# Rotary embedding on one core: float32 transfers on SyncE's queue, rotated in place in five buffers

## The chip, the cores and the metric

The kernel runs on one core of a Trainium2 chip. The metric is the device time of one execution in microseconds (us); the median of eleven runs before the change is 322.9 us, with 321.63 the lowest and 323.37 the highest. Five engines of the core matter here: VectorE (DVE in the profile), ScalarE (ACT), GpSimd (POOL), SyncE (SP), and the 16 DMA engines that move data between HBM and SBUF. TensorE does nothing in this kernel.

## The reference

A rotary position embedding. Each head of 64 numbers is split into two halves, and the halves are rotated by the angle of their place in the sequence:

```python
batch, seq_len, num_heads, head_dim = (8, 2048, 16, 64)
# x: (8, 2048, 16, 64) float32; cos, sin: (2048, 32) float32
x1 = x[..., :head_dim // 2]
x2 = x[..., head_dim // 2:]
out1 = x1 * cos - x2 * sin
out2 = x1 * sin + x2 * cos
return np.concatenate([out1, out2], axis=-1).astype(np.float32)
```

The input and the output are 67.11 MB each; each table is 0.26 MB. Each number of x is used once.

## The kernel before

The work is cut into 16 tiles: two halves of the sequence (1024 rows each) by eight batches, with the half of the sequence as the outer loop. In a tile each of the 128 partitions holds J = 8 consecutive rows of the sequence, which are 8 x 16 x 64 = 8192 numbers. In HBM these are 32 KB in one piece for each partition.

Lines 37 and 38 load the tables cos and sin into SBUF once, as float16. Then each pass of the loop at line 40 does this:

- Line 44 loads a tile of x into the buffer `xt`. The load is issued from GpSimd's queue (`nc.gpsimd.dma_start`), and the transfer turns float32 into float16 on its way.
- Line 59 multiplies the whole tile by cos into `ot`. Lines 65 and 66 multiply the two halves by sin into `v1` and `v2`. Lines 69 and 70 subtract and add these, in place in `ot`. All five run on VectorE in float16. The table is repeated over the heads by its access pattern.
- Line 72 stores `ot`, again from GpSimd's queue, and the transfer turns float16 into float32.

The pools (lines 29 to 31) keep three buffers of each of `xt`, `ot`, `v1` and `v2`. So a load needs that VectorE has read the tile three before it to the end (line 66 is the last reader), and line 59 needs that the store three before it has landed.

The kernel is written on a framework that places the waits and chooses the order of the instructions on each engine; the order in the text is a wish. Each engine then works its own queue off strictly in order, and an instruction that waits holds up what stands behind it on that engine. A transfer's issue is such an instruction, too. What is issued goes into a DMA queue, and one transfer is spread over all 16 DMA engines.

Of the kernel before, what the change touches and what calls it, by code (L numbers as in the profile page):

```python
# [1 line left out]

# [4 lines left out]


@with_exitstack  # L10
def kernel(
    ctx: ExitStack,
    tc: tile.TileContext,
    x: bass.AP,
    cos: bass.AP,
    sin: bass.AP,
    out: bass.AP,
):
    nc = tc.nc
    f16 = mybir.dt.float16  # L20

    B, S, H, D = x.shape
    Dh = D // 2
    P = nc.NUM_PARTITIONS
    J = 8
    NT = S // (J * P)
    T2 = J * P

    const_pool = ctx.enter_context(tc.tile_pool(name="rope_const", bufs=1))
    io_pool = ctx.enter_context(tc.tile_pool(name="rope_io", bufs=3))  # L30
    tmp_pool = ctx.enter_context(tc.tile_pool(name="rope_tmp", bufs=3))

    cos_src = cos.rearrange("(t p j) d -> p t (j d)", p=P, j=J)
    sin_src = sin.rearrange("(t p j) d -> p t (j d)", p=P, j=J)
    cos_sb = const_pool.tile([P, NT, J * Dh], f16)
    sin_sb = const_pool.tile([P, NT, J * Dh], f16)
    nc.gpsimd.dma_start(out=cos_sb, in_=cos_src)  # L37
    nc.gpsimd.dma_start(out=sin_sb, in_=sin_src)  # L38

    for it in range(NT * B):  # L40
        t, b = divmod(it, B)
        s0 = T2 * t
        xt = io_pool.tile([P, J, H, D], f16)
        nc.gpsimd.dma_start(  # L44
            out=xt,
            in_=x[b, s0 : s0 + T2].rearrange("(p j) h d -> p (j h d)", j=J),
        )

        ot = io_pool.tile([P, J, H, D], f16)
        v1 = tmp_pool.tile([P, J, H, Dh], f16)  # L50
        v2 = tmp_pool.tile([P, J, H, Dh], f16)

        x1 = xt[:, :, :, 0:Dh]
        x2 = xt[:, :, :, Dh:D]

        cos_b = cos_sb[:, t, :].rearrange("p (j d) -> p j d", d=Dh).unsqueeze(2)
        sin_b = sin_sb[:, t, :].rearrange("p (j d) -> p j d", d=Dh).unsqueeze(2)

        nc.vector.tensor_mul(  # L59
            out=ot.rearrange("p j h (e d) -> p j (h e) d", d=Dh),  # L60
            in0=xt.rearrange("p j h (e d) -> p j (h e) d", d=Dh),
            in1=cos_b.to_broadcast([P, J, 2 * H, Dh]),
        )
        sin_bb = sin_b.to_broadcast([P, J, H, Dh])
        nc.vector.tensor_mul(out=v1, in0=x2, in1=sin_bb)  # L65
        nc.vector.tensor_mul(out=v2, in0=x1, in1=sin_bb)  # L66
        o1 = ot[:, :, :, 0:Dh]
        o2 = ot[:, :, :, Dh:D]
        nc.vector.tensor_sub(out=o1, in0=o1, in1=v1)  # L69
        nc.vector.tensor_add(out=o2, in0=o2, in1=v2)  # L70

        nc.gpsimd.dma_start(  # L72
            out=out[b, s0 : s0 + T2].rearrange("(p j) h d -> p (j h d)", j=J),
            in_=ot,
        )


# [1 line left out]
_INS = ['x', 'cos', 'sin']  # L79
_OUTS = [((8, 2048, 16, 64), 'float32')]  # L80


# [23 lines left out]
```

## Time and profile before

| What | us |
|---|---|
| Median of 11 runs | 322.9 |
| The profiled execution, its own time | 323.28 |
| Its span in the profile | 321.0 |
| VectorE busy, 80 instructions | 210.7 |
| VectorE idle ahead of line 59, for loads of x | 93.0 |
| GpSimd idle for line 70 (ahead of a store) | 166.9 |
| GpSimd idle for line 66 (ahead of a load) | 117.6 |
| Issue to landing, loads of x, median | 24.3 |
| Issue to landing, stores, median | 20.4 |

The span is the time from the first to the last instruction that the profile holds; the execution's own time is 2.3 us longer. "Issue to landing" includes the time that a transfer waits behind others in the queue. The profile counts the bytes of a transfer where they are written, so that a load, which becomes float16, counts 2 MB and a store 4 MB, though both move 4 MB at the HBM. A rate of some 215 GB/s in a stretch of loads and of some 430 GB/s in a stretch of stores are thus the same rate at the HBM.

### The profile page before, as it was taken

How to read it: one execution, taken by the hardware profiler on the slowest of the kernel's cores; microseconds unless marked ns; L12 is line 12 of the kernel's file. 1: busy time of each engine (PE TensorE's matmuls, PEld its weight loads, DVE VectorE, ACT ScalarE, POOL GpSimd, SP SyncE). 2: the span in 40 equal slices, each digit the busy share in tenths (PEclk: the TensorE clock that was granted, in tenths of full speed). 3: DMA queues.
4: the chain of work that ended last, by engine and by line, in shares of the span. 5: the costliest groups of instructions: out<-in, count | busy, mean ns of one | idle time of the engine just before them, and what ended most of it. 6: DMA issues, size and time to landing. Idle time of an engine off the chain costs nothing.

```text
span 321.0 us, 191 instructions
## 1 busy us (share of the span) xinstructions
DVE 210.7 (66%) x80; POOL 18.9 (6%) x38
## 2 busy tenths in 40 slices
DVE  0079999980009999995003999999100799999800
POOL 4001000011000100002000000000200010000000
DMA  6999999999999999999999999999999999999994
GB/s 88 210 206 227 210 276 425 441 437 421 337 216 212 223 212 359 441 416 449 437 239 225 212 214 234 421 437 433 425 402 212 216 220 214 294 437 421 449 433 196
DMA packets 5154, 100.94 MB, mean 314 GB/s; under 512 B 545, under 2 KB 1057, under 8 KB 1057
## 3 DMA queue, kind: packets, MB, share of 16 engines
q0 software_dynamic: 5152, 100.93, 100.1%
q14 instruction: 2, 0.01, 0.0%
HBM read 67.63 MB, written 67.11 MB: 420 GB/s over the span
## 4 chain that ended last, share of the span: by engine, by line
DVE 45%; DMA 27%; issue 20%; POOL 2%; POOLq 0%; DVEq 0%; PEldq 0%
DMA xt<-in_x_dram 27%; DVE ot L59 16%; DVE v L66 8%; DVE v L65 8%; DVE ot L70 8%; DVE ot L69 4%; POOL out_dram L72 1%; POOL cos_sb L37 0%; POOL sin_sb L38 0%; POOLq L101 0%; POOL xt L44 0%; POOLq L72 0%; DVEq L59 0%; PEldq L101 0%; POOLq L44 0%
## 5 line engine op out<-in xcount | busy, mean ns | idle before, releaser
L59 DVE TENSOR_TENSOR ot<-xt,cos_sb 128x8192 f16<-128x8192 f16 x16 | 70.7, 4421 | 93.0 <-DMA xt<-in_x_dram 92.9
L66 DVE TENSOR_TENSOR v<-xt,sin_sb 128x4096 f16<-128x4096 f16 x16 | 36.6, 2285 | 0.0
L69 DVE TENSOR_TENSOR ot<-ot,v 128x4096 f16<-128x4096 f16 x16 | 36.6, 2285 | 0.0
L70 DVE TENSOR_TENSOR ot<-ot,v 128x4096 f16<-128x4096 f16 x16 | 36.6, 2285 | 0.0
L65 DVE TENSOR_TENSOR v<-xt,sin_sb 128x4096 f16<-128x4096 f16 x16 | 36.6, 2284 | 0.0
L72 POOL DMA_DIRECT2D out_dram<-ot x16 | 8.6, 536 | 166.9 <-DVE ot L70 166.9
L44 POOL DMA_DIRECT2D xt<-in_x_dram x16 | 8.6, 549 | 117.6 <-DVE v L66 117.6
L37 POOL DMA_DIRECT2D cos_sb<-in_cos_dram x1 | 0.8, 827 | 0.8 <-PEq L101 0.8
L38 POOL DMA_DIRECT2D sin_sb<-in_sin_dram x1 | 0.7, 728 | 0.0
L90 POOL MEMSET const-float32-0.0<- 128x1 f32 x1 | 0.1, 99 | 0.2 <-issue 0.2
L90 POOL MEMSET const-bfloat16-1.0<- 128x1 bf16 x1 | 0.1, 102 | 0.0
L90 POOL MEMSET const-float32-1.0<- 128x1 f32 x1 | 0.1, 99 | 0.0
L90 POOL MEMSET const-uint8-127<- 128x1 uint8 x1 | 0.1, 99 | 0.0
## 6 DMA issues: line engine op xcount, KB each, us to landing
out_dram<-ot POOLq DMA_DIRECT2D x16, 4096.0 KB, 20.4
xt<-in_x_dram POOLq DMA_DIRECT2D x16, 2048.0 KB, 24.3
cos_sb<-in_cos_dram POOLq DMA_DIRECT2D x1, 128.0 KB, 3.3
sin_sb<-in_sin_dram POOLq DMA_DIRECT2D x1, 128.0 KB, 3.1
```

Of the source, the lines that this page charges most:

```text
L37: nc.gpsimd.dma_start(out=cos_sb, in_=cos_src)
L38: nc.gpsimd.dma_start(out=sin_sb, in_=sin_src)
L44: nc.gpsimd.dma_start(out=xt, in_=x[b, s0 : s0 + T2].rearrange("(p j) h d -> p (j h d)", j=J),)
L59: nc.vector.tensor_mul(out=ot.rearrange("p j h (e d) -> p j (h e) d", d=Dh), in0=xt.rearrange("p j h (e d) -> p j (h e) d", d=Dh), in1=cos ...
L65: nc.vector.tensor_mul(out=v1, in0=x2, in1=sin_bb)
L66: nc.vector.tensor_mul(out=v2, in0=x1, in1=sin_bb)
L69: nc.vector.tensor_sub(out=o1, in0=o1, in1=v1)
L70: nc.vector.tensor_add(out=o2, in0=o2, in1=v2)
L72: nc.gpsimd.dma_start(out=out[b, s0 : s0 + T2].rearrange("(p j) h d -> p (j h d)", j=J), in_=ot,)
L90: nc = _bacc.Bacc("TRN2", target_bir_lowering=False, num_devices=1)
```

## The change

All transfers are now plain float32 copies, issued from SyncE's queue. The conversion to float16 and back is done by ScalarE in SBUF. A partition holds J = 16 consecutive rows of a batch's sequence (64 KB in HBM), and a unit is half of these, JU = 8 rows (32 KB for each partition); there are 16 units, two for each batch. A unit is computed in two pieces of JC = 4 rows.

- `load` brings a unit into one of five float32 buffers `xf` (NBUF = 5). Four loads are issued ahead, and the tables are loaded as float32 behind the first of them and turned into float16 by ScalarE.
- `narrow` (ScalarE) copies a piece into a float16 tile, of which there are three. `rotate` (VectorE) does the five operations of before on half as many numbers; the product with cos, the difference and the sum are now written in place into this tile. `widen` (ScalarE) copies the result back as float32 into the same place of `xf`.
- The narrowing of the next piece stands ahead of the rotation of this one in the text.
- When both pieces of unit u are done, the text issues the load of unit u + 4, and then the store of unit u out of its `xf`. Unit u + 4 takes the buffer of unit u - 1, whose store must have landed.

```diff
-    J = 8
-    NT = S // (J * P)
-    T2 = J * P
+    J = S // P
+    JU = 8
+    JC = 4
+    NBUF = 5
...
-    io_pool = ctx.enter_context(tc.tile_pool(name="rope_io", bufs=3))
-    tmp_pool = ctx.enter_context(tc.tile_pool(name="rope_tmp", bufs=3))
+    io_pool = ctx.enter_context(tc.tile_pool(name="rope_io", bufs=NBUF))
+    half_pool = ctx.enter_context(tc.tile_pool(name="rope_half", bufs=3))
+    tmp_pool = ctx.enter_context(tc.tile_pool(name="rope_tmp", bufs=1))
...
-    nc.gpsimd.dma_start(out=cos_sb, in_=cos_src)
-    nc.gpsimd.dma_start(out=sin_sb, in_=sin_src)
...
-        xt = io_pool.tile([P, J, H, D], f16)
-        nc.gpsimd.dma_start(
-            out=xt,
-            in_=x[b, s0 : s0 + T2].rearrange("(p j) h d -> p (j h d)", j=J),
-        )
...
+    def load(u):
+        b, j0 = units[u]
+        xf = io_pool.tile([P, JU, H, D], f32)
+        nc.sync.dma_start(out=xf.rearrange("p j h d -> p (j h d)"), in_=rows(x, b, j0))
+        return xf
 
+    def store(u, xf):
+        b, j0 = units[u]
+        nc.sync.dma_start(out=rows(out, b, j0), in_=xf.rearrange("p j h d -> p (j h d)"))
...
+    def narrow(c):
+        xt = half_pool.tile([P, JC, H, D], f16)
+        nc.scalar.copy(out=xt.rearrange("p j h d -> p (j h d)"), in_=piece(c))
+        halves[c] = xt
...
+    def rotate(c):
...
+        nc.vector.tensor_mul(out=v1, in0=x2, in1=sin_b)
+        nc.vector.tensor_mul(out=v2, in0=x1, in1=sin_b)
+        xw = xt.rearrange("p j h (e d) -> p j (h e) d", d=Dh)
+        nc.vector.tensor_mul(out=xw, in0=xw, in1=cos_b)
+        nc.vector.tensor_sub(out=x1, in0=x1, in1=v1)
+        nc.vector.tensor_add(out=x2, in0=x2, in1=v2)
...
+    def widen(c):
+        xt = halves.pop(c)
+        nc.scalar.copy(out=piece(c), in_=xt.rearrange("p j h d -> p (j h d)"))
...
+    for u in range(NBUF - 1):
+        tiles[u] = load(u)
+        if u == 0:
+            nc.sync.dma_start(out=sin_f, in_=sin.rearrange("(p j) d -> p j d", j=J))
+            nc.sync.dma_start(out=cos_f, in_=cos.rearrange("(p j) d -> p j d", j=J))
+            nc.scalar.copy(out=sin_sb, in_=sin_f)
+            nc.scalar.copy(out=cos_sb, in_=cos_f)
 
+    narrow(0)
+    for c in range(n * per):
+        if c + 1 < n * per:
+            narrow(c + 1)
+        rotate(c)
+        widen(c)
+        if c % per == per - 1:
+            u = c // per
+            if u + NBUF - 1 < n:
+                tiles[u + NBUF - 1] = load(u + NBUF - 1)
+            store(u, tiles[u])
...
-        nc.gpsimd.dma_start(
-            out=out[b, s0 : s0 + T2].rearrange("(p j) h d -> p (j h d)", j=J),
-            in_=ot,
-        )
```

More of the change, by code (lines that the diff above doesn't have):

```diff
@@ L20 @@
     f16 = mybir.dt.float16
+    f32 = mybir.dt.float32
     B, S, H, D = x.shape
@@ L24 @@
     P = nc.NUM_PARTITIONS
-    J = 8
-    NT = S // (J * P)
-    T2 = J * P
+    J = S // P
+    JU = 8
+    JC = 4
+    NBUF = 5
     const_pool = ctx.enter_context(tc.tile_pool(name="rope_const", bufs=1))
-    io_pool = ctx.enter_context(tc.tile_pool(name="rope_io", bufs=3))
-    tmp_pool = ctx.enter_context(tc.tile_pool(name="rope_tmp", bufs=3))
-    cos_src = cos.rearrange("(t p j) d -> p t (j d)", p=P, j=J)
-    sin_src = sin.rearrange("(t p j) d -> p t (j d)", p=P, j=J)
-    cos_sb = const_pool.tile([P, NT, J * Dh], f16)
@@ L36 @@
[L36 to L42, printed above, removed]
-        xt = io_pool.tile([P, J, H, D], f16)
-        nc.gpsimd.dma_start(
-            out=xt,
-            in_=x[b, s0 : s0 + T2].rearrange("(p j) h d -> p (j h d)", j=J),
-        )
-        ot = io_pool.tile([P, J, H, D], f16)
-        v1 = tmp_pool.tile([P, J, H, Dh], f16)
-        v2 = tmp_pool.tile([P, J, H, Dh], f16)
+    io_pool = ctx.enter_context(tc.tile_pool(name="rope_io", bufs=NBUF))
@@ new lines, with rows @@
+    half_pool = ctx.enter_context(tc.tile_pool(name="rope_half", bufs=3))
+    tmp_pool = ctx.enter_context(tc.tile_pool(name="rope_tmp", bufs=1))
+    cos_f = const_pool.tile([P, J, Dh], f32)
+    sin_f = const_pool.tile([P, J, Dh], f32)
+    cos_sb = const_pool.tile([P, J, Dh], f16)
+    sin_sb = const_pool.tile([P, J, Dh], f16)
+    units = [(b, j0) for b in range(B) for j0 in range(0, J, JU)]
+    def rows(t, b, j0):
+        return t[b].rearrange("(p j) h d -> p j (h d)", j=J)[:, j0 : j0 + JU, :].rearrange(
+            "p j f -> p (j f)"
+        )
@@ new lines, in load, with piece @@
+    def load(u):
[6 more added lines that the diff above has]
+        nc.sync.dma_start(out=rows(out, b, j0), in_=xf.rearrange("p j h d -> p (j h d)"))
+    n = len(units)
+    per = JU // JC
+    tiles = {}
+    halves = {}
+    def piece(c):
+        u, k = divmod(c, per)
+        return tiles[u][:, k * JC : (k + 1) * JC, :, :].rearrange("p j h d -> p (j h d)")
@@ L53 @@
+    def narrow(c):
[3 more added lines that the diff above has]
+    def rotate(c):
+        u, k = divmod(c, per)
+        j0 = units[u][1] + k * JC
+        js = slice(j0, j0 + JC)
+        xt = halves[c]
+        v1 = tmp_pool.tile([P, JC, H, Dh], f16)
+        v2 = tmp_pool.tile([P, JC, H, Dh], f16)
         x1 = xt[:, :, :, 0:Dh]
         x2 = xt[:, :, :, Dh:D]
-        cos_b = cos_sb[:, t, :].rearrange("p (j d) -> p j d", d=Dh).unsqueeze(2)
@@ L57 @@
[L57 to L62, printed above, removed]
-        )
[L64 to L72, printed above, removed]
-            out=out[b, s0 : s0 + T2].rearrange("(p j) h d -> p (j h d)", j=J),
-            in_=ot,
-        )
+        sin_b = sin_sb[:, js, :].unsqueeze(2).to_broadcast([P, JC, H, Dh])
+        cos_b = cos_sb[:, js, :].unsqueeze(2).to_broadcast([P, JC, 2 * H, Dh])
+        nc.vector.tensor_mul(out=v1, in0=x2, in1=sin_b)
+        nc.vector.tensor_mul(out=v2, in0=x1, in1=sin_b)
```

## The prediction

> **What bounds the kernel now.** I read the page first (sections 1 to 3), then busy time by windows, then the landing times of the loads, then the timeline of the queue. The page:
>
> ```profile
> span 321.0 us, 191 instructions
> DVE 210.7 (66%) x80; POOL 18.9 (6%) x38
> ...
> DMA  6999999999999999999999999999999999999994
> ...
> q0 software_dynamic: 5152, 100.93, 100.1%
> ...
> HBM read 67.63 MB, written 67.11 MB: 420 GB/s over the span
> ```
>
> VectorE works 66% of the span, but the row of slices shows the DMA engines at nine tenths or more from the second slice to the last but one. One queue carries all of it, with 100.1% of the 16 engines' time. So the transfers set the end, and the work is 134.7 MB at the HBM side. The idle time of VectorE is the mirror of that:
>
> ```profile
> L59 DVE TENSOR_TENSOR ot<-xt,cos_sb 128x8192 f16<-128x8192 f16 x16 | 70.7, 4421 | 93.0 <-DMA xt<-in_x_dram 92.9
> L66 DVE TENSOR_TENSOR v<-xt,sin_sb 128x4096 f16<-128x4096 f16 x16 | 36.6, 2285 | 0.0
> ```
>
> The price of one transfer comes from places where only one kind runs. First a stretch of stores alone and the last microseconds (columns: window, length, busy time of VectorE and GpSimd, clock, DMA share, GB/s), then the landing times of the three loads issued together at 71.62:
>
> ```profile
> 60.00:70.00 10.00, 10.00 (x5) 0.00 (x0) 1.00 1.04 439
> ...
> 316.00:317.00 1.00, 0.00 (x0) 0.00 (x0) 1.00 0.64 262
> 317.00:318.00 1.00, 0.00 (x0) 0.00 (x0) 1.00 0.17 66
> 318.00:319.00 1.00, 0.00 (x0) 0.00 (x0) 1.00 0.01 0
> ```
> ```profile
> DMA to landing us min/median/max: 24.5/33.7/42.9
> ```
>
> A store of 4.194 MB at 439 GB/s is 9.55 us. The loads are issued 0.55 apart and land 9.2 + 0.55 = 9.75 us apart: 430 GB/s, counted at the float32 side. One tile in and out is 19.3 us, sixteen are 308.8. The engines' work ends at about 316.8 (0.64 and 0.17 of the last microseconds), the last store lands at 304.0 + 14.9 = 318.9: 2.1 us between the last data and the semaphore. Another 2.1 lie between that and the end of the span.
>
> The timeline gives the start and the order of the queue:
>
> ```profile
> 1.26 0.83 POOL L37 DMA_DIRECT2D cos_sb<-in_cos_dram  x1 [0.82 <-PEq L101]
> 2.09 0.73 POOL L38 DMA_DIRECT2D sin_sb<-in_sin_dram  x1
> 2.81 1.64 POOL L44 DMA_DIRECT2D xt<-in_x_dram  x3
> ...
> 27.09 0.54 POOL L44 DMA_DIRECT2D xt<-in_x_dram  x1 [22.64 <-DVE v L66]
> ...
> 31.50 0.54 POOL L72 DMA_DIRECT2D out_dram<-ot  x1 [3.87 <-DVE ot L70]
> ```
>
> The first load lands at 2.81 + 15.06 = 17.87 (the chain of waits). From there to 318.9 are 301.05 us for 15 loads and 16 stores, 299.05 by the prices above: 2.0 us of slack in all. The reader is to see two things. First, little is left to win: 308.8 of 321.0 is transfer at full rate. Secondly, the queue is not in the order of the text: the text alternates load and store, the chip runs four loads and then a store. The framework moves an instruction whose operands are late behind later ones that are ready.
>
> **What the Trainium skill says.** "DMA: Bandwidth & Descriptors", section on SWDGE, HWDGE and iDMA: a cast in a transfer can be issued only from GpSimd; a plain one goes from SyncE or ScalarE. Its table of latencies puts the first byte at 0.6 us by hardware and about 1 us by software; here the first table issue at 1.26 shows data from about 2.7. The same page, "Anatomy of one DMA": a fixed 2 us per transfer, most of it the write receipt, and waits happen on the issuing sequencer, not in the DMA engines. The 2.1 us above agree. "SBUF — State Buffer" warns that VectorE can starve descriptor writing for GpSimd's queue. This trace doesn't show it: 439 GB/s with VectorE busy all of 60 to 70. So leaving GpSimd's queue wins nothing there.
>
> **The change part by part.**
>
> *Bytes.* The HBM side is unchanged: 16 transfers in, 16 out, of 32 KB per partition, and the tables. Only the SBUF side doubles. The engines already run at 430 and 439 on the wider side, so I take the same 9.75 and 9.55. Not shown by this trace: a float32-to-float32 load from the hardware queue, with rows 64 KB apart. Bounds: 0.5% faster (no software ring), or loads at the 408.7 GB/s that the skill's DMA page (iDMA part) gives for a load stream from SyncE with 4 KB rows: 10.26 us a load, +8.2 us in all. I take +0.5, since these rows are 32 KB.
>
> *Start.* Load 0 goes first and the tables behind it. SyncE can issue at about 1.3, as GpSimd did; first data 1.0 later (between 0.6 and the 1.4 seen), at 2.3. Tables: 0.52 MB at 430 GB/s, 1.2 us.
>
> *VectorE.* 4421 for 8192 elements and 2285 for 4096 give 0.5215 ns an element and 149 ns fixed, so 2048 take 1217. A piece is 2285 + 4 x 1217 = 7153; 32 pieces, 229 us; a unit, 14.3. Price of the split: 18 us of VectorE, hidden under the 19.3 us of transfers a unit.
>
> *ScalarE.* New: 64 copies of 4096 elements. No row shows one; "ScalarE: Activation LUTs" (cost of the ACTIVATE) gives 186 + 0.833 x 4096 = 3598 ns with immediates: 14.4 us a unit, 230 in all, hidden too. The upper bound that still hides is 19.3 / 4 = 4.8 us. The chain from a load's landing to its store: 3.6 + 2 x 7.15 + 3.6 = 21.5 us, up to about 28 where the narrowing of the next unit stands ahead of the last widening on ScalarE and waits for its load. While a store waits for that, two or three other transfers cover it.
>
> *Buffers and queue.* In place, a buffer is held from the issue of its load to the landing of its store. Load u + 5 must wait for store u. Five buffers are 5 x 19.3 = 96.5 us of round; a round needs 9.75 + 2.1 + 28 + 9.55 + 2.1 + 1, about 53. So on average two buffers wait in the queue and it doesn't run dry, if the order on SyncE is by readiness: stores 1 and 2 are computed (at some 45 and 59 us) before store 0 lands (five loads and a store, about 63), so they'd go ahead of load 5. Its wait is then covered by two stores of 9.55. *Tail:* after load 15 lands, store 15 needs 21.5 us; with stores 12 to 14 still queued (28.7) nothing is lost, with two of them (19.1) some 5 us. I take nothing.
>
> *Sum against the profiled execution:* 2.3 + 1.2 + 308.8 + 2.0 (slack as before) + 0.5 = 314.8, + 2.1 to land, + 2.1 = 319.0 of span, + 2.3 around it (323.28 - 321.0) = 321.3. Profiled before: 323.28, 0.4 above the median; so 320.9, say 321.0. The gain, 2 us, is the start alone: the load no longer stands behind two table issues and their small packets.
>
> **The rivals.**
>
> *A: the queue drains at each reload (slower).* In the text, load u + 4 stands ahead of store u, and waits for store u - 1, the transfer just issued. If SyncE gets them in that order, it stands at the load's wait, with a finished store perhaps behind it, and nothing is left in the DMA queue. Price each: 2.1 to land, 0.1 to wake, 1.0 to first data, 3.2; loads 5 to 15 make 11: +35 us, 356. It decides as soon as the load stands directly behind the store it waits for. For it: the text. Against: the queue before is ordered by readiness; but what was passed there waited for data, not for a buffer, so this isn't proved. Chance 0.18.
>
> *B: the hardware float32 transfers are slower, or the tail is open.* Loads at 408.7 GB/s: 329; the tail: 326; both 334. For it: rows and sides not seen here. Against: the engines sit at one rate whatever the narrow side. Chance 0.27.
>
> *C: ScalarE is the bound.* At 5 us a copy, 20 us a unit instead of 19.3: 16 x 0.7, and the fill, about 14 us: 335. Against: the price of 3.6. Chance 0.05.
>
> *D: the start brings nothing*, because the first load is as late as before for another reason: 323. It lies within my case.
>
> **How the numbers follow.** My case, chance 0.50: 318.5 to 323.5, predicted 321.0. B and C add 0.32, up to 336; A, 0.18, is left out, so the range is 317.5 to 338. A measurement here can tell about 0.2%, 0.65 us, from no change: faster means under 322.25. Of my case 0.38 lies there, 0.10 within, 0.02 above; B gives 0.03 faster and 0.03 same (its small end); the rest is slower. Together 0.41, 0.13, 0.46.
>
> **What would show it.** Right: DMA share near 1 in every slice, VectorE and ScalarE each at 14 to 15 us a unit, first load landed near 14, stores 1 and 2 ahead of load 5 on SyncE. Wrong: SyncE's wait for the store in eleven places with a dip in the DMA row (A); a stretch of loads under 420 GB/s, or a gap before the last store (B); ScalarE copies over 4.8 us and VectorE waiting for them (C).

## The result, and the profile after

The changed kernel takes 321.42 us (median of 13 runs, 319.49 to 322.18) against 323.13 us for the kernel before (48 runs). The ratio is 0.9952, with a 95% interval of 0.994 to 0.9964: 0.5% faster, 1.7 us. The profiled execution took 321.42 us, 1.8 more than its span.

These lines of the page of the changed kernel answer to the ones shown of before:

```profile
span 319.6 us, 387 instructions
DVE 223.1 (70%) x160; ACT 229.3 (72%) x67; POOL 0.2 (0%) x4
...
DMA  8999999999999999999999999999999999999993
...
q1 hardware_dynamic: 4896, 134.74, 98.3%
...
HBM read 67.63 MB, written 67.11 MB: 422 GB/s over the span
...
L92 ACT CAST xf<-xt 128x4096 f32<-128x4096 f16 x32 | 115.3, 3604 | 51.0 <-DVE xt L88 28.0
L69 ACT CAST xt<-xf 128x4096 f16<-128x4096 f32 x32 | 114.5, 3601 | 19.7 <-DMA xf<-in_x_dram 19.7
L83 DVE TENSOR_TENSOR v<-xt,sin_sb 128x2048 f16<-128x2048 f16 x32 | 39.1, 1223 | 71.6 <-ACT xt L69 54.7
```

The DMA engines are still busy throughout, from the first slice (8 tenths, 6 before) to the last but one. VectorE and ScalarE both work over 220 us under that. The order of SyncE's queue, in its timeline (start, duration from the first to the last of the group, count):

```profile
0.73 0.39 SPq L51 DMA_DIRECT2D xf<-in_x_dram  x1
...
2.11 2.01 SPq L51 DMA_DIRECT2D xf<-in_x_dram  x4
34.82 18.17 SPq L56 DMA_DIRECT2D out_dram<-xf  x2
63.94 10.11 SPq L51 DMA_DIRECT2D xf<-in_x_dram  x2
74.14 3.97 SPq L56 DMA_DIRECT2D out_dram<-xf  x2
...
260.19 40.88 SPq L56 DMA_DIRECT2D out_dram<-xf  x4
```

The queue runs in twos, not in the order of the text: stores 0 and 1 stand ahead of load 5. Load 5 is issued at 63.94, when store 0 has landed, and store 1 is then the DMA engines' work. The wait is long (195 us over eleven loads), but the DMA engines have work behind it, so that it costs nothing.

The end of the span is new (columns: window, length, busy VectorE, ScalarE, GpSimd, clock, DMA share, GB/s):

```profile
314.00:315.00 1.00, 0.00 (x0) 0.00 (x0) 0.00 (x0) 1.00 0.31 131
315.00:316.00 1.00, 0.00 (x0) 0.00 (x0) 0.00 (x0) 1.00 0.16 66
316.00:317.00 1.00, 0.00 (x0) 0.00 (x0) 0.00 (x0) 1.00 0.00 0
317.00:318.00 1.00, 0.00 (x0) 0.00 (x0) 0.00 (x0) 1.00 0.08 33
```

The trace also has the start and the duration of every packet. A large transfer is 128 packets, which I call rows: 32 KB each on the float32 side, eight on each engine, one behind the other. The windows count a row where it starts. By their ends, the median engine is done with its last row at 315.15 and the last engine at 318.35. Every transfer lands in 16 increments of its semaphore, which I take as one for each DMA engine, and the trace has the time of each. From these increments I call *lag* the time by which the last engine is behind the median one. For the first load and the last store (us from the start of the span):

```
                first load            last store             span
                median   last         median   last   lag
before          17.20    17.87        317.93   318.87  0.93   321.0
changed         12.58    12.75        315.38   318.77  3.39   319.6
```

So the first load lands 5.1 us earlier, and nearly all of that is gone when the last store lands. The tables, now behind that load, take back 1.3 (they land at 13.40 and 14.07, and load 1 is late by that). The lag takes 3.0: from the first load to the last store it grows by 3.2 us, where it grew by 0.3 before. The median engine's rows take the remaining 0.7. What is won in the span is mostly the time after the last landing: 0.9 instead of 2.1 us.

### The profile page after: what moved, and what is told of

Same layout as the page of the kernel before. It is cut to its first block, busy times and chain, and to the rows that moved or that the text cites. A ratio compares the mean times of both kernels' runs of the same rounds, so it can differ in the third digit from the quotient of the medians.

```text
span 319.6 us, 387 instructions
## 1 busy us (share of the span) xinstructions
DVE 223.1 (70%) x160; ACT 229.3 (72%) x67; POOL 0.2 (0%) x4
## 4 chain that ended last, share of the span: by engine, by line
DMA 39%; DVE 6%; ACT 6%; issue 2%; DVEq 0%; SPq 0%; ACTq 0%
DMA out_dram<-xf 33%; DMA xf<-in_x_dram 6%; ACT xt L69 3%; ACT xf L92 2%; DVE xt L86 2%; DVE xt L87 1%; DVE v L83 1%; DVE v L84 1%; DVEq L138 0%; DVE xt L88 0%; SPq L51 0%; SPq L56 0%; ACTq L92 0%
## 5 line engine op out<-in xcount | busy, mean ns | idle before, releaser
L92 ACT CAST xf<-xt 128x4096 f32<-128x4096 f16 x32 | 115.3, 3604 | 51.0 <-DVE xt L88 28.0
L69 ACT CAST xt<-xf 128x4096 f16<-128x4096 f32 x32 | 114.5, 3601 | 19.7 <-DMA xf<-in_x_dram 19.7
L83 DVE TENSOR_TENSOR v<-xt,sin_sb 128x2048 f16<-128x2048 f16 x32 | 39.1, 1223 | 71.6 <-ACT xt L69 54.7
L86 DVE TENSOR_TENSOR xt<-xt,cos_sb 128x4096 f16<-128x4096 f16 x32 | 73.3, 2292 | 1.2
L87 DVE TENSOR_TENSOR xt<-xt,v 128x2048 f16<-128x2048 f16 x32 | 39.2, 1225 | 1.1
L84 DVE TENSOR_TENSOR v<-xt,sin_sb 128x2048 f16<-128x2048 f16 x32 | 39.0, 1218 | 0.0
L88 DVE TENSOR_TENSOR xt<-xt,v 128x2048 f16<-128x2048 f16 x32 | 39.0, 1218 | 0.0
```

Of the source, the lines that this page charges most:

```text
L69: nc.scalar.copy(out=xt.rearrange("p j h d -> p (j h d)"), in_=piece(c))
L83: nc.vector.tensor_mul(out=v1, in0=x2, in1=sin_b)
L84: nc.vector.tensor_mul(out=v2, in0=x1, in1=sin_b)
L86: nc.vector.tensor_mul(out=xw, in0=xw, in1=cos_b)
L87: nc.vector.tensor_sub(out=x1, in0=x1, in1=v1)
L88: nc.vector.tensor_add(out=x2, in0=x2, in1=v2)
```

## The experiments

The first four ran side by side, as did the next four and the last two.

**The same kernel again.** No edit.

> The changed kernel once more. If the lag of single DMA engines (the last of the 16 lands the last store 3.4 us behind the median one, 0.9 in the kernel before) belongs to the kernel, it is seen again, above 2 us, and the ratio to before stays 0.994 to 0.996. If it was chance in that one profile, the lag is 1 us or less and this span is some 2 us shorter than 319.6.

321.38 us, ratio 0.9943 (0.9931 to 0.9955). The lag at the last store is 3.70 us. So the lag belongs to the kernel and is no accident of one profile.

**The order of the text.** Every store is held behind the load that precedes it in the text.

```diff
     def store(u, xf):
         b, j0 = units[u]
-        nc.sync.dma_start(out=rows(out, b, j0), in_=...)
+        with tc.issue_after(last[-1]):
+            nc.sync.dma_start(out=rows(out, b, j0), in_=...)
```

> Each store is held behind the load that stands ahead of it in the text, so that load u+4 follows directly on the store it waits for. If the queue's order by readiness is what keeps the DMA engines fed (my theory), each of the loads 5 to 15 costs about 3.2 us: +35, 356 us. If a store's landing is hidden some other way, the time stays within 3 us of 321.4.

361.95 us, 40.6 more than the changed kernel beside it. SyncE's timeline and the busy shares of one unit in this kernel:

```profile
157.47 0.33 SPq L51 DMA_DIRECT2D xf<-in_x_dram  x1
157.85 0.42 SPq L58 DMA_DIRECT2D out_dram<-xf  x1
180.70 0.33 SPq L51 DMA_DIRECT2D xf<-in_x_dram  x1
```
```profile
157.00:160.00 3.00, 0.36 (x1) 3.00 (x2) 0.00 (x0) 1.00 0.62 175
160.00:170.00 10.00, 9.90 (x8) 6.32 (x2) 0.00 (x0) 1.00 0.98 367
170.00:180.00 10.00, 3.68 (x3) 6.60 (x3) 0.00 (x0) 1.00 0.97 419
180.00:183.00 3.00, 2.06 (x2) 3.00 (x2) 0.00 (x0) 1.00 0.59 175
```

A load and a store are issued together, and nothing more for 23.23 us, although two transfers that follow on each other land 2 x 9.68 = 19.36 us apart (stores in the kernel before). The DMA share dips to 0.6 at both ends of the unit shown. The difference, 3.87 us, is the price of this order for each unit, and eleven of them are 42.6 us.

The packets of the unit shown split it in two halves. The median engine is idle for 1.8 us between its last row of a store and its first row of the next load (1.7 to 2.0 in the other drains, once 2.8). In that lie the wait for the engine that is last, 0.35 us from its last row to the semaphore, and 0.96 from the issue to the first row. The other half is slow rows: an engine's sixteen take 21.4 us instead of 16 x 1.21 = 19.4. The first row behind the drain takes 1.84 in the median, and the last two of the load, ahead of the store, 1.64 and 2.14. In the changed kernel rows are slow on all engines like this only at the start and at the first turn to stores; why they are slow isn't shown.

Since each drain also brings the engines together (the lag of the last store is 0.70), a little comes back. So it is the order by readiness that keeps the changed kernel from being 13% slower.

**The software queue.** All transfers from GpSimd, still float32.

```diff
-        nc.sync.dma_start(...)
+        nc.gpsimd.dma_start(...)
```

> The changed kernel with all transfers issued from GpSimd instead of SyncE, still float32 on both sides. If the start, the end and the lag of engines belong to the hardware queue: first load lands near 16 instead of 12.75, the lag at the end falls to about 1 us, the end after the last landing grows from 0.8 to 2.1, together 322 to 324 us. If they belong to the float32 buffers and the order of the transfers: the same as the changed kernel, 321.4, with the lag above 2 us.

325.24 us, ratio 1.0069 (1.0054 to 1.0083), slower than either expectation. The first load lands at 13.96 instead of 12.75, earlier than the 16 that I gave, and 2.1 us lie behind the last landing instead of 0.9. Both belong to the queue. The lag doesn't: it is 4.59 us here.

**The kernel before, first load first.** The two table loads are moved into the loop, behind the load of the first tile. Nothing else changes: GpSimd's queue, casts in the transfers.

```diff
-    nc.gpsimd.dma_start(out=cos_sb, in_=cos_src)
-    nc.gpsimd.dma_start(out=sin_sb, in_=sin_src)
...
+        if it == 0:
+            nc.gpsimd.dma_start(out=cos_sb, in_=cos_src)
+            nc.gpsimd.dma_start(out=sin_sb, in_=sin_src)
```

> The kernel before with its first load ahead of the two tables. If the late first load (17.87) is the two table issues ahead of it, it lands near 15.5 and the time falls by 1.5 to 2.5 us, to about 321. If it is the software queue's own start, it lands above 17 and the time falls by less than 0.6.

320.62 us, ratio 0.9924 (0.9912 to 0.9936). In its timeline the first load is issued at 1.26, and VectorE starts at 14.59 instead of 17.97:

```profile
1.26 0.67 POOL L41 DMA_DIRECT2D xt<-in_x_dram  x1 [0.81 <-PEq L101]
1.92 0.72 POOL L46 DMA_DIRECT2D cos_sb<-in_cos_dram  x1
...
14.59 4.43 DVE L59 TENSOR_TENSOR ot<-xt,cos_sb 128x8192 f16<-128x8192 f16 x1 [14.59 <-DMA cos_sb<-in_cos_dram]
```

The load lands at 13.82, 4.05 us earlier for an issue 1.55 earlier, and earlier than the 15.5 that I gave. This move of two lines alone brings more than the whole change (1.7 us beside it).

The runs side by side split the change: 323.06, first load first, -2.44; float32 on the same queue, with ScalarE, five buffers in place and the new order, +4.62; SyncE's hardware queue, -3.86; together 321.38. Of the 4.62, the lag is 4.1 in the two profiles (4.59 against 0.46 at the last store).

**32 KB rows.** The changed kernel with the tiling of before: 1024 consecutive rows of the sequence in a unit, so that a partition's 32 KB follow on its neighbour's.

```diff
-    units = [(b, j0) for b in range(B) for j0 in range(0, J, JU)]
+    units = [(b, j0) for j0 in range(0, J, JU) for b in range(B)]
...
-        return t[b].rearrange("(p j) h d -> p j (h d)", j=J)[:, j0 : j0 + JU, :]...
+        s0 = j0 * P
+        return t[b, s0 : s0 + JU * P].rearrange("(p j) h d -> p (j h d)", j=JU)
```

> The changed kernel with the tiling of before: a unit is 1024 consecutive rows, so a partition's 32 KB lie next to its neighbour's in HBM, with no 64 KB pitch; queue, buffers, order and engines as in the changed kernel. If the lag of single DMA engines comes of the 64 KB rows, it falls to about 1 us at the end and the time to some 319. If it comes of the float32 side in SBUF or of loads and stores taking turns in twos, it stays above 2 us and the time at 321.4.

321.44 us, ratio 0.9962 (0.9948 to 0.9977), lag 2.75 us. The pitch of the rows isn't the cause. That the lag is smaller than 3.39 means little: the profile is of this kernel's fastest execution (320.70), and over the three profiles of the two kernels the time follows the lag (320.70 with 2.75, 321.42 with 3.39, 321.65 with 3.70).

**Three buffers.** `NBUF = 3`.

> NBUF 3 instead of 5. By the prediction's round of 53 us for a buffer against 3 x 19.3 = 58 us of transfers, three buffers would just do: no more than 5 us slower if the queue's order stays good. If the wait for the store's landing is exposed once in each unit as in the run in text order (some 3.9 us each), 360 us or more.

354.5 us, ratio 1.0993. Both numbers that I gave are missed; the first theory is wrong. SyncE waits 195 us for ScalarE's widening ahead of the stores. From 110.65 to 153.90, and in each pair after that, two units take 43.3 us, so three buffers turn once in 65 us, not in 53.

**More work for ScalarE.** One more copy of 2048 numbers ahead of each widening, into a scratch tile.

```diff
     def widen(c):
+        ex = tmp_pool.tile([P, 2048], f16)
+        nc.scalar.copy(out=ex, in_=halves[c].rearrange("p j h d -> p (j h d)")[:, 0:2048])
         xt = halves.pop(c)
```

> One more ScalarE copy of 2048 numbers ahead of each widening, into a scratch tile, about 1.9 us each, 61 us of ScalarE work in all: a unit is then 18.2 us of ScalarE against 19.3 of transfers. If ScalarE is hidden as predicted, the time stays within 1 us of 321.4. If it is on the path, up to 61 us are added.

343.83 us, 22.4 more than the changed kernel: 60.6 us of work were added and a good third shows, nearly all of it at the end. Windows of this kernel (DMA share in the last column but one):

```profile
260.00:280.00 20.00, 10.87 (x9) 15.78 (x6) 0.00 (x0) 1.00 0.99 428
280.00:300.00 20.00, 16.06 (x12) 19.67 (x7) 0.00 (x0) 1.00 0.76 328
300.00:320.00 20.00, 10.87 (x10) 14.74 (x6) 0.00 (x0) 1.00 0.55 236
320.00:341.00 21.00, 4.54 (x3) 8.48 (x3) 0.00 (x0) 1.00 0.47 200
```

Until 280 the DMA engines are full. Then the last load has landed, the arithmetic is some units behind, and the last stores come 12.6, 16.1 and 23.1 us apart instead of 9.7. So ScalarE is hidden in the loop, but its backlog comes due at the tail. How near the changed kernel is to that is seen in its own timeline of ScalarE:

```profile
127.59 7.11 ACT L69 CAST xt<-xf 128x4096 f16<-128x4096 f32 x2
138.38 3.61 ACT L92 CAST xf<-xt 128x4096 f32<-128x4096 f16 x1 [3.68 <-issue]
141.89 3.60 ACT L69 CAST xt<-xf 128x4096 f16<-128x4096 f32 x1
145.40 3.60 ACT L92 CAST xf<-xt 128x4096 f32<-128x4096 f16 x1
...
159.71 3.60 ACT L92 CAST xf<-xt 128x4096 f32<-128x4096 f16 x1 [3.42 <-DVE xt L88]
163.22 7.11 ACT L69 CAST xt<-xf 128x4096 f16<-128x4096 f32 x2
```

Two units are a closed round of 35.6 us: inside it they overlap, but its last widening (159.71) stands ahead of the next narrowing (163.22). That is 17.8 us a unit against 19.3 of transfers, not 14.4. The last store is issued at 300.7, when the store ahead of it still moves data for about 5 us (it lands at 305.7 on the median engine).

**Two queues.** Stores from ScalarE's hardware queue, loads from SyncE's.

```diff
-        nc.sync.dma_start(out=rows(out, b, j0), in_=...)
+        nc.scalar.dma_start(out=rows(out, b, j0), in_=...)
```

> Stores issued from ScalarE's hardware queue, loads from SyncE's, so that both kinds can be in the DMA engines at once. If the order within one queue makes the lag of single engines, or costs anything, the time falls below 320.5; if the engines' rate sets the end, it stays at 321 to 322.

319.25 us, ratio 0.99 (0.9882 to 0.9918): the lowest median here, ahead of both given kernels, with 424 GB/s over a span of 317.5 us. The lag at the last store is 1.57 us; the median engine lands it at 315.04, 0.34 earlier than in the changed kernel, and the last engine at 316.61, 2.16 earlier:

```profile
313.00:314.00 1.00, 0.00 (x0) 0.00 (x0) 0.00 (x0) 1.00 1.21 524
314.00:315.00 1.00, 0.00 (x0) 0.00 (x0) 0.00 (x0) 1.00 0.23 98
315.00:316.00 1.00, 0.00 (x0) 0.00 (x0) 0.00 (x0) 1.00 0.00 0
```

So it is the lag that falls; the median engine hardly changes. While loads and stores run at once, the stores land with a lag of 2.1 to 2.7 us and the loads with one of 0.3 to 1.1; behind the last load it is 1.3 to 1.8. The run changes two things together: that there are two queues, and that loads and stores mix row by row (of the rows that start between 100 and 103 us, 17 are of loads and 29 of stores). It doesn't tell which of them counts.

**Alternating, and groups of four.** The order of SyncE's queue is fixed by dependencies without a wait, first to store u, load u + 4, store u + 1 and so on, then to four loads and four stores.

```diff
+    for a, b in zip(order, order[1:]):
+        tc.add_manual_dep(dmas[b], dmas[a].name, ...)
```

> The queue's order fixed to store u, load u+4, store u+1, and so on: one change from load to store in every unit (11 behind load 4) instead of one in two units, and each load still has one store between it and the store that it waits for. If single DMA engines lose time where the queue turns from loads to stores, the lag at the end grows to 5 us or more and the time to 323 or more. If the lag has nothing to do with the turns, it stays at 3.5 us and the time at 321.4.

340.51 us, but most of it for a reason that I hadn't expected. The fixed order changed the framework's order on ScalarE too: from 92 us on the two narrowings of a unit always stand behind the last widening of the unit before. From its timeline:

```profile
262.78 7.11 ACT L74 CAST xt<-xf 128x4096 f16<-128x4096 f32 x2
...
284.08 7.11 ACT L74 CAST xt<-xf 128x4096 f16<-128x4096 f32 x2
```

A unit takes 21.3 us, more than the 19.3 of its transfers; the backlog is paid at the tail, as in the run before (the DMA share is 0.49 between 300 and 320). The lag before that tail, at store 13, is 4.28 us.

> The queue's order fixed to groups of four loads and four stores, as the kernel before runs: four turns from loads to stores instead of seven. If the turns make the lag, it falls to 2 us or less and the time to about 320. If the float32 side in SBUF makes it, it stays above 3 us and the time at 321.4.

322.78 us, ratio 1.0004 (0.9994 to 1.0015). Here too the last two stores wait for the arithmetic. The lag at store 13 is 2.59 us. For the times the two runs thus say nothing on the lag. At store 13 the lag seems to follow the number of turns from loads to stores (2.59 with groups of four, 3.42 and 3.74 in the two profiles of the changed kernel, 4.28 alternating). But between stores 12 and 13 the changed kernel has an event that isn't a turn (the fetch at 293.5 in the next section), which adds 0.8 to its lag and falls later in the two others. At store 12 the lag is 2.57 with four turns, 2.62 and 2.96 with seven, and 4.29 with twelve. In these profiles four and seven turns thus don't differ, and that fewer turns than seven make less lag isn't shown.

**Where the lag comes from.** A row takes 1213 ns (1227 before), nearly always. This table has the rows that start after 60 us and take 150 ns more than that:

```
                 slow rows   their excess, us   lag, last store
before                1             0.21               0.93
before_x_first        1             0.21               0.46
changed              10             4.28               3.39
again                17             6.12               3.70
rows_32k             29             8.31               2.75
gp_queue             41            15.26               4.59
two_queues            3             1.16               1.57
groups_of_4           9             3.64               2.59 (store 13)
alternate            48            17.15               4.28 (store 13)
```

The kernels with much lag are those with more than three slow rows, but their number doesn't give the size of the lag: that counts one engine against the median, and the trace doesn't say which engine a row is on.

In the changed kernel slow rows stand at two kinds of places. Two rows, at 92.4 and 293.8, start 0.31 us behind the start of a fetch of instructions, which the DMA engines also do (92.09 and 293.49, 309 ns each). The third fetch, at 179.07, has none. Between store 12 and store 13 only the second of these falls, and there the lag goes from 2.62 to 3.42. The fetch's own 0.31 and the 0.35 by which its row is slow make up 0.66 of that 0.80. The others stand at 168.6 to 169.1, 208.3, 246.5 and 276.0 to 276.3, in the last rows of a load behind which the queue turns to stores (at 276, from load 15 to store 12). One to three engines lose up to 0.8 us there. At the turn near 131 no row is slow, and 92.4 is beside a turn as well. An engine doesn't catch up while the queue is full, since each has its own eight rows of every transfer. Where the queue drains, the engines come together again: in both runs with a fixed order the last store has a lag of 0.09. With two queues, the only slow rows are those behind the three fetches.

## Why the prediction was right, point by point

The forecast was 321.0, the measured median is 321.42. The direction and the size of the gain were right, but the sum met the time by chance. Three of its terms were too large, by 2.3 us together (the first data 0.6, the time behind the last landing 1.2, the time around the span 0.5). Two were too small, by 2.4 (0.9 from the first data to the median engine's last row, 1.5 from there to the last landing).

- *The bound.* Right: the transfers at full rate. Rival B's slower loads didn't come. Between the first load and the last store the median engine needs 302.8 us, tables included, for the 300.25 that the prices 9.75 and 9.55 give with the 1.2 of the tables. The price of a store was a little low: it came from the 439 GB/s of a window of 10 us, which counts whole rows where they start, while stores that follow on each other land 9.68 apart in the kernel before. With 9.7 for both kinds, more than half of the "slack" is gone.
- *Start: "SyncE can issue at about 1.3", first data at 2.3.* Too late. SyncE issues at 0.73, the first packets run at 1.74, and the load lands at 12.75 where the sum put it near 14. The reason given, that the load no longer stands behind two table issues, holds: that move alone made the old kernel 2.44 us faster, more than the 2 us that I gave the whole change.
- *"2.1 us between the last data and the semaphore".* A wrong reading, and the mis-sized term on the other side. The window view let the work end at about 316.8. By the packets of the kernel before, the median engine's last row ends at 317.57, the last engine's at 318.50, and the semaphore is complete at 318.87: 0.37 to land, and 0.93 for the engine that is last; the other 0.8 come of the view, which counts rows where they start. So the 2.1 is no fixed cost of a transfer, as the prediction took it. In the changed kernel it is 0.42 and 3.20, and I had no term for a slow engine.
- *"+ 2.1" behind the last landing and 2.3 around the span.* 0.9 and 1.8. These I carried over from a program that ends on GpSimd's software queue; the run with the software queue has 2.1 and 2.3 again.
- *Rival A.* Right as to the place and the deciding point; each drain costs 3.87 us, not 3.2, and of other parts. The page "DMA: Bandwidth & Descriptors" of the Trainium skill ("Anatomy of one DMA") puts some 2 us on every transfer, most of it the receipt of the last write. By the packets here the last row of a store ends 0.35 us ahead of the semaphore, an engine is idle for 1.8 in all, and slow rows, which rival A didn't count, bring 2.0. The chance of 0.18 rested on whether a load that waits for a buffer is passed by a store. It is.
- *VectorE and ScalarE.* Their prices were good: 1223 and 2292 ns against 1217 and 2285, 3601 to 3604 against 3598. The step from prices to a unit, "14.4 us a unit", failed: it is 17.8 as ordered and 21.3 in another order. The 21.3 are nearly the chain of 21.5 from a load's landing to its store, with no overlap between units. ScalarE is hidden with far less room than said. For the same reason only store 1, and not "stores 1 and 2", stands ahead of load 5: store 2 was computed at 74 us, not at 59.
- *Buffers: "about 53".* Too small: three buffers turn in 65 us. Five still cover that (96.5 us of transfers), but with less room than said.
- *Tail.* Nothing was lost, as taken, with about 5 us to spare.

Not settled is why a turn from loads to stores slows single rows with float32 on the SBUF side in one queue, and not in the kernel before. The rows' pitch, the kind of queue and groups of two instead of four are excluded as the sole cause by runs. What is left of the difference to the kernel before is float32 instead of float16 on the SBUF side, with ScalarE's copies and the five buffers; no run separates these. With two queues the slow rows at the turns are gone, with float32 on both sides.

## What to carry to other kernels

When the DMA engines are full from start to end, look at the two ends first: which transfer is issued first, and what lies between the last data and the end. Judge a wait on a transfer's landing by what is still queued behind that transfer: here one more transfer of some 9.7 us hid it, and none cost 3.9 us each time, half of it idle and half slow rows behind the drain and at the turn. Don't read the end of the work from a view that counts by windows: the last engine, not the mean, sets it. A stage that is hidden by its mean must also be counted in the order in which it runs, and its backlog is due behind the last load.

## What the runs showed of the hardware that was not expected

- The 16 DMA engines of one queue don't stay together: the last fell behind the median by 2.75 to 4.6 us in 300 us of float32 traffic in one queue, and ended 1.6 behind with loads and stores in two queues. A drained queue brings them together again.
- A fetch of instructions by the DMA engines (309 ns) can leave one engine behind: in the changed kernel 0.8 of the 3.4 us of lag came in the one store in which a fetch fell.
- From the end of the last row to the complete semaphore there are 0.34 to 0.44 us in all kernels here, stores of 4 MB to HBM.
- Two hardware queues were faster than one, 0.99 against 0.9943 and 0.9952 of the time before. The Trainium skill ("DMA: Bandwidth & Descriptors", section "Issuing engines are not separate DMA queues") says that issuing from several engines saves only the sequencer's time. That isn't all here: SyncE's issues take 0.34 us each and the queue never ran dry (from 60 to 310 us the DMA share is 0.98 or more in windows of 10 and 20 us); what differs is the lag.
- The first rows of the changed kernel are slow on nearly every engine, 1.4 to 2.1 us instead of 1.2. So are the last two rows of the load ahead of the first turn to stores (1.84 and 1.64 in the median, at 50 to 52 us). After every drain in the text's order both come again, and cost 2.0 us a unit.
